# Output-projection weight sums formed in DRAM during attention, and no subtraction of weight parts on POOL

## The chip, the cores and the metric

The kernel runs on one core of a Trainium2 chip. The metric is the device time of one execution in microseconds (us); the runs before the change have a median of 803.27 us. One further execution was taken with the hardware profiler; all views below come from it. Engine names: PE is the matrix engine (PEld its weight load), DVE the vector engine, ACT the scalar engine, POOL the general engine, SP the one that only issues transfers. Transfers issued by SP run on queue q1, those issued by POOL on queue q0; both queues share 16 DMA engines.

## The reference, cut to what matters

A hybrid decoder layer for 512 tokens of width 1024: an mLSTM branch and a sparse-attention branch, merged by gates into `y`, an output projection with a residual, then a gated conv-MLP. The change concerns the output projection's weights:

```
y = sigmoid(gm + merge_gate_b[0]) * (hm @ w_up_m) + sigmoid(gn + merge_gate_b[1]) * (on @ w_up_n)
x = x + y @ w_out                      # w_out is 1024 x 1024
h2 = rmsnorm(x, norm2_w)
a, v = jnp.split(h2 @ ffn_w_up, 2, axis=-1)
a = jax.nn.gelu(causal_dwconv(a, ffn_conv_w, ffn_conv_b), approximate=False)
return x + (a * v) @ ffn_w_down
```

## The kernel before, in words

**Products.** Every float32 product is made of three matmuls of a reduced type (fp32r): with each operand split into a high part H and a low part L (the rest), it adds H·H, H·L and L·H (lines 507 to 509 in `mm3`; 567 to 569 in the feature-major projections, 587 to 589 in `up_group`). So every weight is loaded raw, copied to its high part on ACT (L102), and its low part is raw minus high. The class `Weights` does this in halves of 128x1024, in program order. A low half is made in one of four ways: by DVE (L110), by POOL (L110, for the halves in `on_pool`), late by DVE (L53), or, for the halves in `on_dma`, by a second ACT copy with the sign turned (L107) and an accumulating transfer issued by POOL that adds the raw weights to it (L108). Raw weights go through two buffers (`raw`), parts through a ring of four (`whl`); `rawdst` and `dst` give a chunk a place of its own, and `deep` lets one more chunk be loaded ahead.

**Stages.** First the input projections and attention: the rest of the projections (`proj_stream`: gates `gm`, output gates `mo`, `mqk`, gates `gn`) is fed between the pieces of attention and of the mLSTM by `fill`, so that PE always has matmuls. Attention is a loop over 32 pairs of a token tile and a head. Then `un` and `um` multiply the two branches by `w_up_n` and `w_up_m` (8 groups each of 12 matmuls), and their evacuations `evac_un` and `evac_um` on DVE merge them into `gm`, which then holds `y`.

**Output projection.** It takes 7 products of half-size blocks instead of 8. The blocks of `w_out` (512 x 512) are combined before use: T1 = w00 + w01, T2 = T1 + w11, T4 = T2 + w10, T3 = w01 + w11. The activations are combined likewise (s2, s5, s3, s7). PE runs the products in the order P1 (weights w00), P2 (w10), P6 (T2), P5 (T1), P3 (w11), P7 (T3), P4 (T4); each is 24 matmuls. Between them ACT and DVE split activations (`a_split`, L1457 and L1458), POOL adds products into the residual tiles `x` (L1585 to L1610), and DVE and ACT form the second norm (`norm2_sq`, `norm2_x` with the scaling L1561), whose result `junk` PE transposes (`pn`, L491) between P7 and P4. After P4 the first up-projection group (`ff`) begins.

**The sums before.** `wo_sums`, called in the mLSTM's last head, loads the four blocks into four pages of SBUF (L1359, tiles b11, b12, b22, b21) and forms the sums in place by 8 accumulating transfers issued by POOL (L1364). b11 then holds T1, b12 T3, b22 T2, b21 T4. `t_split` splits T1 and T2 while `um` runs (two ACT copies, L1462 and L1464, and an accumulating transfer on POOL's queue, L1465). T3 and T4 are split by `Weights`. POOL subtracts the low halves of the second half of T4 and of the first two up-projection halves (`LOWS`).

**What sets the order.** Each engine runs its instructions in the order of the program text; a wait stops everything behind it on that engine, and transfers of one queue are issued in order. Nothing is reordered by a planner; the table `PLAN` gives amounts of filler and engine choices, and the change does not touch it.

Of the kernel before, what the change touches and what calls it, by code (L numbers as in the profile page):

```python
# [15 lines left out]
P = 128  # L16
# [129 lines left out]
def FL(key, default):  # L146
    return PLAN.get(key, default)
# [30 lines left out]
def body(ctx, tc, I, out, dbg=None):  # L178
# [38 lines left out]
    def page_r(name):  # L217
        return page(name, F32R)
# [4 lines left out]
    def s4(name, dt=F32):  # L223
        return ar.tile([P, 1024], dt, name=name, tag="s4", bufs=6)
# [16 lines left out]
    def act4(tiles, k, a=0, b=S):  # L241
        return v4(tiles[k // 4])[:, k % 4, a:b]

    T = {}
    done = set()

    def cp(key, default, dst, src):
# [41 lines left out]
    def wo_block(r, c):  # L289
        return w_out[r * 512:r * 512 + 512, c * 512:c * 512 + 512].rearrange("(k p) n -> p k n", p=P)  # L290

    WB = {}
    for nm, rc, pg in (("b11", (0, 0), None), ("b21", (1, 0), None), ("b22", (1, 1), None), ("T3", None, "b12"),
                       ("T4", None, "b21")):
        W.deep.add(len(W.chunks))
        if pg:
            W.rawdst[len(W.chunks)] = lambda name, pg=pg: T[pg]
        WB[nm] = W.add((4, 512), [] if pg else [(lambda v: v, wo_block(*rc))],
                       [lambda v, a=a: v[:, a:a + 2] for a in (0, 2)])
    F_FA, F_FV = [], []  # L300
    for c in range(0, DFF, 256):
# [555 lines left out]
    def evac_un(m, a):  # L857
        g = T["gn"][m // 4][:, m % 4, :]
        dve.tensor_mul(g, g, a)
# [204 lines left out]
    def att_out(i, acc):  # L1064
# [6 lines left out]
        act.activation(oh, av, AF.Copy)  # L1071
        dve.tensor_sub(ol, av, oh)

    def attention():
        its = [(i, h) for i in range(NT) for h in range(8)]
        f1 = [FL(f"f1_{k}", v) for k, v in enumerate((1950, 1300, 1000, 1000)) for _ in range(8)]
        f2 = [FL(f"f2_{k}", v) for k, v in enumerate((0, 0, 1300, 1300)) for _ in range(8)]
        f3 = [FL(f"f3_{k}", v) for k, v in enumerate((650, 1000, 300, 300)) for _ in range(8)]
        pcs = {0: pc0}
        rows, step = rows_b(), None  # L1080
        sv, nmx = att_scores(0, 0)
        Pt, Pv, den = att_exp(0, 0, sv, nmx)
        fill(FL("z7", 1950))
        att_scale(0, 0, Pv, den)
        acc = po("on0")
        cmp_out(acc, pcs[0])
        fill(FL("z9", 1300))
        for n, (i, h) in enumerate(its):
            nxt = its[n + 1] if n + 1 < len(its) else None
            if nxt:  # L1090
# [36 lines left out]
            if nxt:  # L1127
                Pt, Pv, den = nPt, nPv, nden
# [222 lines left out]
    fill.until(done, "CONV")  # L1351
    assert "ROWS" in done

    def wo_sums():

        blocks = (("b11", (0, 0)), ("b12", (0, 1)), ("b22", (1, 1)), ("b21", (1, 0)))
        for nm, rc in blocks:
            T[nm] = opage(nm)
            nc.sync.dma_start(T[nm].rearrange("p (k n) -> p k n", k=4), wo_block(*rc))  # L1359
        for d, src in (("b11", (0, 1)), ("b12", (1, 1)), ("b22", "b11"), ("b21", "b22")):  # L1360
            dv = T[d].rearrange("p (k n) -> p k n", k=4)
            sv = T[src].rearrange("p (k n) -> p k n", k=4) if isinstance(src, str) else wo_block(*src)
            for k in (0, 2):
# [73 lines left out]
    x1p = [lpage("x1_0")]  # L1437
    x1 = [x1p[0][:, t * 1024:(t + 1) * 1024] for t in range(2)]
    s7t = s4("s7t")
    TH = {nm: [s4(f"{nm}H{i}", F32R) for i in range(2)] for nm in ("T1", "T2")}  # L1440
    nw2 = s4("nw2")

    A = {nm: page_r("A" + nm) for nm in ("a11", "a12")}
    TL = {nm: page_r(nm + "L") for nm in ("T1", "T2")}
    LO, HI = slice(0, 256), slice(256, 512)

    def Y(g, k0, n, t):  # L1450
# [6 lines left out]
        act.activation(h, src, AF.Copy)  # L1457
        dve.tensor_sub(l, src, h)  # L1458

    def t_split(nm, i):  # L1460
        src = T["b11" if nm == "T1" else "b22"][:, i * 1024:i * 1024 + 1024]
        act.activation(TH[nm][i], src, AF.Copy)  # L1462
        l = TL[nm][:, i * 1024:i * 1024 + 1024]
        act.activation(l, TH[nm][i], AF.Copy, scale=-1.0)  # L1464
        pool.dma_start(l, src, accum_op=ALU.add)  # L1465

    S7 = s7t.rearrange("p (k t) -> p k t", k=4)

    def s52(e, k0):
        e.tensor_sub(Y(0, k0, 2, HI), Y(0, k0, 2, HI), Y(1, k0, 2, HI))  # L1470
        e.tensor_sub(Y(0, k0, 2, LO), Y(0, k0, 2, LO), Y(0, k0, 2, HI))

    def evac_um(m, a):
        g = T["gm"][m // 4][:, m % 4, :]
        dve.tensor_mul(g, g, a)
# [133 lines left out]
    for a in range(2):  # L1609
        pool.tensor_sub(xh(2 + a, 0), xh(2 + a, 0), V[a])  # L1610
    A["a22"] = page_r("Aa22")
    for k in range(4):
        for a in range(2):
            wo("P5", a, (k,))
        if k == 1:
            norm2_sq(0, 0, 0)
            norm2_sq(1, 0, 0)
        elif k == 2:
            a_split("a22", Y(1, 0, 4, HI), 0, 4)
            for a in range(2):  # L1620
                norm2_e(a)
    for a in range(2):
# [24 lines left out]
    for a in range(2):
# [345 lines left out]
```

## Time and profile before

| | |
|---|---|
| median of 3 runs | 803.27 us (802.63 to 804.4) |
| the profiled execution | 802.46 us |
| its span, first to last instruction | 800.8 us |
| mean granted PE clock | 0.981 |
| PE busy | 771.3 us (96%) |
| DVE, ACT, POOL busy | 490.8, 393.0, 246.8 us |
| DMA | 140.56 MB, of it 45.09 MB on q0 |

Times in a view are us from the span's start, mean durations of one instruction ns. A row of the chain of waits gives start, duration and what filled it; a row of the timeline adds shapes, a count and in brackets the idle time before with its releaser; a row of the table of stretches gives busy time (and count) of each engine, the granted PE clock, the mean busy share of the 16 DMA engines and GB/s. A busy PE is not PE at its peak: at half the granted clock a matmul takes twice as long and still counts as busy.

### The profile page before, as it was taken

The numbers are of one execution on the slowest core, as the hardware profiler recorded it, in microseconds if no ns is written. First come the engines' busy times: TensorE is split into PE (matmuls) and PEld (weight loads), VectorE is DVE, ScalarE is ACT, GpSimd is POOL, SyncE is SP. The second block draws the span as 40 slices with busy tenths as digits, with TensorE's granted clock in tenths as the row PEclk, the third lists the DMA queues.
The fourth block names the chain that finished last, engine by engine and source line by source line (L and its number), as shares of the span: only waits on it lengthen the run. The fifth ranks groups of instructions, "written<-read, shape, count | busy, mean of one in ns | idle before, by whom it ended". The sixth has DMA issues, their size and how long they took to land.

```text
span 800.8 us, 10584 instructions
## 1 busy us (share of the span) xinstructions
PE 771.3 (96%) x3991; PEld 637.5 (80%) x3991; DVE 490.8 (61%) x844; ACT 393.0 (49%) x655; POOL 246.8 (31%) x251
## 2 busy tenths in 40 slices
PE   8999999999999999978876999999999999999998
PEld 7897887788888778867665988888888888888786
DVE  7486876776557575436558745554554544565866
ACT  6363565555565765746373443333333333355452
POOL 3320221210111222123348008855554443200600
PEclk9999999999999999997988999999999999999999
DMA  7974278755564577699983467675555444585472
GB/s 237 322 185 132 34 154 143 145 99 99 87 128 66 103 158 132 188 275 253 289 211 66 154 234 262 230 256 210 191 177 191 182 155 157 189 284 184 129 230 102
DMA packets 99459, 140.56 MB, mean 176 GB/s; under 512 B 6831, under 2 KB 72783, under 8 KB 98000
## 3 DMA queue, kind: packets, MB, share of 16 engines
q1 hardware_dynamic: 65662, 94.66, 35.3%
q0 software_dynamic: 33600, 45.09, 27.5%
q8 instruction: 31, 0.51, 0.3%
q14 instruction: 20, 0.16, 0.1%
q10 hardware_dynamic: 146, 0.14, 0.0%
HBM read 100.03 MB, written 15.73 MB: 145 GB/s over the span
## 4 chain that ended last, share of the span: by engine, by line
PE 85%; DMA 6%; DVE 4%; ACT 2%; issue 2%; POOL 0%; DVEq 0%; ACTq 0%; SPq 0%; POOLq 0%
PE ff L1676 10%; PE ff L1678 10%; PE ff L1677 10%; PE P L508 4%; PE P L509 4%; PE P L507 4%; DMA raw<-in_w_up_m_dram 3%; PE on L1061 3%; PE ptp L1050 2%; PE gn L567 2%; PE gm L567 2%; PE gm L569 2%; PE gm L568 2%; PE gn L569 2%; PE gn L568 2%; DMA raw<-in_w_out_dram 2%
## 5 line engine op out<-in xcount | busy, mean ns | idle before, releaser
L110 DVE TENSOR_TENSOR whl<-raw,whl 128x1024 fp32r<-128x1024 f32 (+1 forms) x102 | 132.0, 1304 | 144.8 <-ACT whl L102 144.6
L102 ACT ACTIVATE whl<-raw 128x1024 fp32r<-128x1024 f32 (+2 forms) x142 | 143.1, 1012 | 138.0 <-PE ff L1678 55.7
L1676 PE MATMUL ff<-h2H,whl 128*128 128x512 f32 (+1 forms) x376 | 141.3, 376 | 0.0
L1677 PE MATMUL ff<-h2L,whl 128*128 128x512 f32 (+1 forms) x376 | 141.2, 375 | 0.0
L1678 PE MATMUL ff<-h2H,whl 128*128 128x512 f32 (+1 forms) x376 | 141.2, 375 | 0.0
L108 POOL DMA_DIRECT2D whl<-raw x35 | 48.7, 1390 | 206.7 <-ACT whl L107 182.0
L1678 PEld LDWEIGHTS ff<-h2H,whl 128*128 128x128 f32 x376 | 70.8, 188 | 12.9
L1677 PEld LDWEIGHTS ff<-h2L,whl 128*128 128x128 f32 x376 | 70.8, 188 | 12.8
L1676 PEld LDWEIGHTS ff<-h2H,whl 128*128 128x128 f32 x376 | 70.8, 188 | 12.6
L1035 ACT ACTIVATE P<-sp,nmx 128x128 f32<-128x128 f32 (+3 forms) x64 | 33.1, 523 | 36.7 <-DVE nmx L1026 36.2
L1743 ACT ACTIVATE ct<-ct 128x512 f32<-128x512 f32 x22 | 13.9, 633 | 53.8 <-DVE ct L1741 53.8
L107 ACT ACTIVATE whl<-raw 128x1024 fp32r<-128x1024 f32 x35 | 36.7, 1049 | 0.0
L1026 DVE TENSOR_REDUCE nmx<-sp 128x2 f32<-128x256 f32 (+3 forms) x32 | 26.2, 819 | 16.3 <-PE sp L1023 16.2
L507 PE MATMUL P<-whl,g 128*128 128x512 f32 x88 | 34.2, 389 | 0.0
L508 PE MATMUL P<-whl,g 128*128 128x512 f32 x88 | 34.2, 389 | 0.0
L509 PE MATMUL P<-whl,g 128*128 128x512 f32 x88 | 34.2, 389 | 0.0
L1741 DVE SCALAR_TENSOR_TENSOR ct<-ff,vcol,ct 128x511 f32<-128x511 f32 (+1 forms) x44 | 32.7, 743 | 2.2 <-ACT ct L1739 1.4
L1749 ACT ACTIVATE g<-ct 128x512 fp32r<-128x512 f32 x22 | 13.9, 632 | 36.4 <-DVE ct L1753 21.4
L252 DVE COPY P<-ptp 128x256 f32<-128x256 f32 (+1 forms) x32 | 17.7, 553 | 18.4 <-PE ptp L1050 18.3
L1750 DVE TENSOR_TENSOR g<-ct,g 128x512 fp32r<-128x512 f32 x22 | 15.4, 699 | 21.9 <-ACT g L1749 21.9
L508 PE MATMUL P<-whl,sb 128*128 128x512 f32 (+1 forms) x68 | 26.3, 386 | 1.5 <-DVE whl L110 1.4
L567 PE MATMUL gm<-hTH,whl 128*128 128x512 f32 x64 | 26.6, 416 | 0.0
(453 smaller groups left out, 1847.7 us busy)
## 6 DMA issues: line engine op xcount, KB each, us to landing
raw<-in_ffn_w_up_dram SPq DMA_DIRECT2D x22, 1024.0 KB, 5.2
whl<-raw POOLq DMA_DIRECT2D x35, 512.0 KB, 5.7
raw<-in_w_in_dram SPq DMA_DIRECT2D x16, 1024.0 KB, 5.1
st<-in_ffn_w_down_dram SPq DMA_DIRECT2D x11, 1024.0 KB, 7.7
td<-st POOLq DMA_DIRECT2D x11, 1024.0 KB, 4.2
raw<-td SPq DMA_DIRECT2D x22, 512.0 KB, 5.5
raw<-in_ffn_w_down_dram SPq DMA_DIRECT2D x11, 512.0 KB, 3.9
b<-in_w_out_dram SPq DMA_DIRECT2D x4, 1024.0 KB, 8.1
```

The costliest lines, as they stand in the source:

```text
L102: nc.scalar.activation(h, src, AF.Copy)
L107: nc.scalar.activation(l, src, AF.Copy, scale=-1.0)
L108: nc.gpsimd.dma_start(l, src, accum_op=ALU.add)
L110: (nc.gpsimd if n in self.on_pool else nc.vector).tensor_sub(l, src, h)
L507: pe.matmul(o, aH, bH, start=start, stop=False)
L508: pe.matmul(o, aH, bL, start=False, stop=False)
L509: pe.matmul(o, aL, bH, start=False, stop=stop)
L567: pe.matmul(acc, H[:, k, :], hh, start=(k == 0), stop=False)
L1035: act.activation(Pv[:, y], sv[:, y], AF.Exp, bias=nmx[:, y:y + 1], accum_out=den[:, y:y + 1])
L1676: pe.matmul(acc[:, a:b], H[:, k, :], hh, start=(k == 0), stop=False)
L1677: pe.matmul(acc[:, a:b], H[:, k, :], hl, start=False, stop=False)
L1678: pe.matmul(acc[:, a:b], L[:, k, :], hh, start=False, stop=(k == KD - 1))
```

## The change

- **Sums in DRAM.** Four DRAM tiles `tw` (tags wT1 to wT4) take the sums. In each of the first 16 steps of attention SP copies a quarter of a block, 128 rows of 512 numbers, from DRAM to DRAM; in steps 4 to 19 POOL issues an accumulating transfer that adds a quarter of another block, or of an earlier sum, to it (`block_sums`). The 4 loads of L1359 and the 8 accumulating transfers of L1364 go. `wo_sums` now only loads T1 and T2; T3 and T4 are loaded by `Weights` as raw chunks into pages.
- **T1 and T2** are split by one ACT copy and one DVE subtraction each half, without a transfer, and earlier: T1 after `un` groups 2 and 3, T2 after `un` group 6 and `um` group 0.
- **No low halves on POOL.** Those of T4's second half and of the first two up-projection halves are made by the second ACT copy and an accumulating transfer. T4's parts get two pages of their own (`W.dst`), outside the ring, so the parts after them move up in the ring.
- **Places.** T4's halves are made before P5 and in P5, the two up-projection halves in P3 and in the second norm. The two subtractions of `s52` for the first features go from POOL to DVE.

```
-    for nm, rc, pg in (("b11", (0, 0), None), ("b21", (1, 0), None), ("b22", (1, 1), None), ("T3", None, "b12"),
-                       ("T4", None, "b21")):
-        W.deep.add(len(W.chunks))
-        if pg:
-            W.rawdst[len(W.chunks)] = lambda name, pg=pg: T[pg]
-        WB[nm] = W.add((4, 512), [] if pg else [(lambda v: v, wo_block(*rc))],
+    tw = {nm: dram.tile([P, 2112], F32, name="w" + nm, tag="w" + nm) for nm in ("T1", "T2", "T3", "T4")}
...
+    for nm, rc in (("b11", (0, 0)), ("b21", (1, 0)), ("b22", (1, 1)), ("T3", None), ("T4", None)):
+        if nm != "b11":
+            W.deep.add(len(W.chunks))
+        if not rc:
+            W.rawdst[len(W.chunks)] = lambda name: opage(name)
+        WB[nm] = W.add((4, 512), [(lambda v: v, wo_block(*rc) if rc else twv(nm))],
...
-    LOWS = (WB["T4"][1], F_FA[0], F_FA[1])
-    W.on_pool = {T_B[c] for c in range(4) if FL(f"q2_pb{c}", (1, 0, 0, 0)[c])} | set(LOWS)
+    W.on_pool = {T_B[c] for c in range(4) if FL(f"q2_pb{c}", (1, 0, 0, 0)[c])}
...
-                    ("UN", F_UN), ("UM", F_UM), ("WO", WB["b11"] + WB["b21"][:1] + WB["b22"] + WB["T3"] + WB["T4"][:1])):
+                    ("UN", F_UN), ("UM", F_UM), ("WO", WB["b11"] + WB["b21"][:1] + WB["b22"] + WB["T3"] + WB["T4"] + F_FA[:2])):
...
+    for i in WB["T4"]:
+        W.dst[i] = page_r
...
+        if m in (2, 3, 6):                                   # in evac_un
+            t_split("T2" if m == 6 else "T1", m % 2)
...
+    def block_sums(n):                                       # called at the start of attention's step n
+        names = ("T1", "T3", "T2", "T4")
+        k = n % 4
+        if n < 16:
+            nc.sync.dma_start(twv(names[n // 4])[:, k], wo_block(*((0, 0), (0, 1), (1, 1), (1, 0))[n // 4])[:, k])
+        if 4 <= n < 20:
+            z = n // 4 - 1
+            src = (wo_block(0, 1), wo_block(1, 1), twv("T1"), twv("T2"))[z]
+            pool.dma_start(twv(names[z])[:, k], src[:, k], accum_op=ALU.add)
...
+    def t_split(nm, i):
...
+        act.activation(TH[nm][i], src, AF.Copy)
+        dve.tensor_sub(TL[nm][:, i * 1024:i * 1024 + 1024], src, TH[nm][i])
...
     def wo_sums():
-        blocks = (("b11", (0, 0)), ("b12", (0, 1)), ("b22", (1, 1)), ("b21", (1, 0)))
-        for nm, rc in blocks:
+        for nm in ("T1", "T2"):
             T[nm] = opage(nm)
-            nc.sync.dma_start(T[nm].rearrange("p (k n) -> p k n", k=4), wo_block(*rc))
-        for d, src in (("b11", (0, 1)), ("b12", (1, 1)), ("b22", "b11"), ("b21", "b22")):
...
-                pool.dma_start(dv[:, k:k + 2], sv[:, k:k + 2], accum_op=ALU.add)
+            nc.sync.dma_start(T[nm], tw[nm][:, 0:2048])
...
-        act.activation(l, TH[nm][i], AF.Copy, scale=-1.0)    # the old t_split
-        pool.dma_start(l, src, accum_op=ALU.add)
...
         elif m == 5:                                         # in evac_um
-            t_split("T2", 1)
-            s52(pool, 0)
+            s52(dve, 0)
...
+    W.ensure(WB["T4"][0])                                    # before P5; T4[1] in P5 after k == 2,
     for k in range(4):                                       # the first up-projection half in P3 after k == 1,
         for a in range(2):                                   # the second in the second norm
             wo("P5", a, (k,))
```

In the order fences the number in a name is that of its buffer or tile: whl48 and whl49 are w00's parts, whl50 and whl51 w10's, 52 and 53 w11's, 54 and 55 T3's, 56 and 57 T4's, 58 and 59 the first two up-projection halves.

The first place is POOL from the last low half of `w_up_n` to the loads of the residual tiles, that is the `un` and `um` stage; before:

```order
L108 DMA whl41_3291<-raw20_3051 128x4x256
L1364 DMA b11_3390<-in_w_out_dram 128x2x512 x2
L1364 DMA b12_3392<-in_w_out_dram 128x2x512 x2
L1364 DMA b22_3394<-b11_3390 128x1024 x2
L1364 DMA b21_3396<-b22_3394 128x1024 x2
L1465 DMA T1L_3559<-b11_3390 128x1024
L1480 TENSOR_TENSOR s7t_3551<-gm0_1198 128x512
L1465 DMA T1L_3559<-b11_3390 128x1024
L108 DMA whl48_3612<-raw24_3523 128x1024
L1485 TENSOR_TENSOR s7t_3551<-gm0_1198 128x512
L1465 DMA T2L_3560<-b22_3394 128x1024
L108 DMA whl49_3654<-raw24_3523 128x1024
```

and of the change:

```order
L108 DMA whl41_3327<-raw20_3087 128x4x256
L1493 TENSOR_TENSOR s7t_3587<-gm0_1202 128x512
L108 DMA whl48_3636<-raw24_3554 128x1024
L1497 TENSOR_TENSOR s7t_3587<-gm0_1202 128x512
L108 DMA whl49_3675<-raw24_3554 128x1024
L108 DMA whl50_3715<-raw25_3634 128x1024
L1522 DMA x1_0_3586<-in_x_dram 128x1024 x2
L1522 DMA x1_1_3756<-in_x_dram 128x1024 x2
```

Eleven accumulating transfers ahead of w00's second half (whl49) are gone from POOL's queue, and with the later T2L transfer and the two `s52` subtractions nothing stands between w10's half and the residual loads.

The second place is POOL at the end of the output projection, from the last residual subtraction to the stores of the residual; before:

```order
L1610 TENSOR_TENSOR x1_1_3734<-x1_1_3734,V_3862 128x512 x2
L108 DMA whl56_3927<-b21_3396 128x1024
L110 TENSOR_TENSOR whl57_3954<-b21_3396,whl57_3954 128x1024
L110 TENSOR_TENSOR whl58_3982<-raw29_3804,whl58_3982 128x1024
L110 TENSOR_TENSOR whl59_3997<-raw29_3804,whl59_3997 128x1024
L1564 DMA x1d_3549<-x1_0_3550 128x1024 x2
```

and of the change:

```order
L1620 TENSOR_TENSOR x1_1_3756<-x1_1_3756,V_3886 128x512 x2
L108 DMA whl56_3899<-raw28_3782 128x1024
L108 DMA whl57_3931<-raw28_3782 128x1024
L108 DMA whl58_3959<-raw29_3828 128x8x128
L108 DMA whl59_3993<-raw29_3828 128x8x128
L1574 DMA x1d_3585<-x1_0_3586 128x1024 x2
```

Three subtractions on POOL have become three accumulating transfers in the same place of its queue.

The third place is POOL in attention, where whl20 to whl23 are low halves of the gates `gm`, whl24 and whl25 of `mo`, and wT1, wT3 and wT2 are the DRAM sums; before:

```order
L108 DMA whl20_1311<-raw10_1159 128x8x128
L108 DMA whl21_1406<-raw10_1159 128x8x128
L108 DMA whl22_1506<-raw11_1309 128x8x128
L108 DMA whl23_1597<-raw11_1309 128x8x128
L108 DMA whl24_1693<-raw12_1504 128x8x128
L1172 TENSOR_SCALAR mrowC_1734<-onesf_98 32x512
L108 DMA whl25_1790<-raw12_1504 128x8x128
```

and of the change:

```order
L108 DMA whl20_1317<-raw10_1163 128x8x128
L1091 DMA wT1_85<-in_w_out_dram 128x512
L108 DMA whl21_1416<-raw10_1163 128x8x128
L1091 DMA wT1_85<-in_w_out_dram 128x512 x3
L108 DMA whl22_1522<-raw11_1315 128x8x128
L1091 DMA wT3_87<-in_w_out_dram 128x512 x2
L108 DMA whl23_1617<-raw11_1315 128x8x128
L1091 DMA wT3_87<-in_w_out_dram 128x512 x2
L108 DMA whl24_1717<-raw12_1520 128x8x128
L1192 TENSOR_SCALAR mrowC_1758<-onesf_102 32x512
L1091 DMA wT2_86<-wT1_85 128x512 x2
L108 DMA whl25_1818<-raw12_1520 128x8x128
```

One to three adding transfers now stand between two low halves, and each waits for its copy, which stands behind a raw load in SP's queue.

More of the change, by code (lines that the diff above doesn't have):

```diff
@@ L242, in act4 @@
         return v4(tiles[k // 4])[:, k % 4, a:b]
-    T = {}
+    T, TH, TL = {}, {}, {}
     done = set()
@@ L292, in body, with twv @@
     WB = {}
-    for nm, rc, pg in (("b11", (0, 0), None), ("b21", (1, 0), None), ("b22", (1, 1), None), ("T3", None, "b12"),
-                       ("T4", None, "b21")):
-        W.deep.add(len(W.chunks))
-        if pg:
-            W.rawdst[len(W.chunks)] = lambda name, pg=pg: T[pg]
-        WB[nm] = W.add((4, 512), [] if pg else [(lambda v: v, wo_block(*rc))],
+    tw = {nm: dram.tile([P, 2112], F32, name="w" + nm, tag="w" + nm) for nm in ("T1", "T2", "T3", "T4")}
+    def twv(nm):
+        return tw[nm][:, 0:2048].rearrange("p (k n) -> p k n", k=4)
+    for nm, rc in (("b11", (0, 0)), ("b21", (1, 0)), ("b22", (1, 1)), ("T3", None), ("T4", None)):
[4 more added lines that the diff above has]
+        WB[nm] = W.add((4, 512), [(lambda v: v, wo_block(*rc) if rc else twv(nm))],
                        [lambda v, a=a: v[:, a:a + 2] for a in (0, 2)])
@@ L1089, in attention @@
             nxt = its[n + 1] if n + 1 < len(its) else None
+            block_sums(n)
             if nxt:
@@ L1352, in body @@
     assert "ROWS" in done
+    def t_split(nm, i):
+        if not i:
+            TH[nm] = [s4(f"{nm}H{z}", F32R) for z in range(2)]
+            TL[nm] = page_r(nm + "L")
+        src = T[nm][:, i * 1024:i * 1024 + 1024]
+        act.activation(TH[nm][i], src, AF.Copy)
+        dve.tensor_sub(TL[nm][:, i * 1024:i * 1024 + 1024], src, TH[nm][i])
     def wo_sums():
-        blocks = (("b11", (0, 0)), ("b12", (0, 1)), ("b22", (1, 1)), ("b21", (1, 0)))
-        for nm, rc in blocks:
+        for nm in ("T1", "T2"):
             T[nm] = opage(nm)
-            nc.sync.dma_start(T[nm].rearrange("p (k n) -> p k n", k=4), wo_block(*rc))
-        for d, src in (("b11", (0, 1)), ("b12", (1, 1)), ("b22", "b11"), ("b21", "b22")):
-            dv = T[d].rearrange("p (k n) -> p k n", k=4)
-            sv = T[src].rearrange("p (k n) -> p k n", k=4) if isinstance(src, str) else wo_block(*src)
-            for k in (0, 2):
-                pool.dma_start(dv[:, k:k + 2], sv[:, k:k + 2], accum_op=ALU.add)
+            nc.sync.dma_start(T[nm], tw[nm][:, 0:2048])
     T["mq"] = [v4(page_r(f"mq{p}")) for p in range(2)]
@@ L1439, in body @@
     s7t = s4("s7t")
-    TH = {nm: [s4(f"{nm}H{i}", F32R) for i in range(2)] for nm in ("T1", "T2")}
     nw2 = s4("nw2")
     A = {nm: page_r("A" + nm) for nm in ("a11", "a12")}
-    TL = {nm: page_r(nm + "L") for nm in ("T1", "T2")}
     LO, HI = slice(0, 256), slice(256, 512)
@@ L1458, in a_split @@
         dve.tensor_sub(l, src, h)
[L1460 to L1463, printed above, removed]
-        act.activation(l, TH[nm][i], AF.Copy, scale=-1.0)
-        pool.dma_start(l, src, accum_op=ALU.add)
     S7 = s7t.rearrange("p (k t) -> p k t", k=4)
@@ L1477, in evac_um @@
         if m == 0:
-            t_split("T1", 0)
+            t_split("T2", 1)
         elif m == 1:
             pool.tensor_sub(S7[:, 0:2], Y(0, 0, 2, HI), Y(0, 0, 2, LO))
-            t_split("T1", 1)
         elif m == 2:
@@ L1486, in evac_um @@
             a_split("a11", Y(0, 2, 2, LO), 2, 2)
-            t_split("T2", 0)
         elif m == 5:
-            t_split("T2", 1)
-            s52(pool, 0)
+            s52(dve, 0)
         elif m == 6:
@@ L1621, in body @@
                 norm2_e(a)
+            W.ensure(WB["T4"][1])
     for a in range(2):
@@ L1629, in body @@
         if k == 1:
-            W.ensure(WB["T4"][0])
+            W.ensure(ff_ids(0)[0])
     for a in range(2):
@@ L1635, in body @@
         norm2_x(a)
-        if not a:
-            W.ensure(WB["T4"][1])
+        if a:
+            W.ensure(ff_ids(0)[1])
     h2H = [opage_r(f"h2H{i}") for i in range(2)]
@@ L1643, in body @@
                 wo("P7", a, (k,))
-        W.ensure(ff_ids(0)[i])
     for t in range(2):
```

## The prediction

> **What bounds the kernel now.** First the page's busy rows, then what PE waited for.
>
> ```profile
> PE 771.3 (96%) x3991; PEld 637.5 (80%) x3991; DVE 490.8 (61%) x844; ACT 393.0 (49%) x655; POOL 246.8 (31%) x251
> ```
>
> ```profile
> PE pn L491 <- DVE junk L1561: 7.6, 2, 7.2
> PE um L587 <- DVE gn L859: 6.9, 1, 6.9
> PE wP L508 <- DMA whl<-raw: 3.4, 2, 2.1
> PE wP L509 <- DVE As L1458: 2.6, 1, 2.6
> PE wP L507 <- ACT As L1457: 1.6, 1, 1.6
> ```
>
> PE is the bound with 771.3 of 800.8 us. Nearly all its idle time is in these five rows, 22.1 us (total us, times, longest), and all five lie between `un` and the up-projection. So the table of stretches for that part, cut at the waits: `um` waits in the first row, runs in the next two, then P1 and P2, P6 alone, P5, P3 and P7, and last the second norm's transposes with P4.
>
> ```profile
> 355.90:362.90 7.00, 0.11 (x2) 0.03 (x1) 1.90 (x3) 2.96 (x4) 0.00 (x0) 0.66 1.09 259
> 362.90:368.30 5.40, 5.40 (x13) 4.24 (x14) 2.94 (x4) 3.05 (x3) 0.86 (x1) 0.50 1.04 288
> 368.30:384.60 16.30, 16.30 (x73) 13.48 (x72) 11.09 (x14) 11.49 (x13) 10.02 (x11) 1.00 1.07 231
> 384.60:401.10 16.50, 13.12 (x49) 9.99 (x48) 7.75 (x10) 2.62 (x4) 4.55 (x6) 0.90 1.04 313
> 401.10:406.60 5.50, 5.50 (x25) 4.33 (x24) 1.22 (x1) 4.65 (x5) 0.88 (x1) 1.00 0.51 153
> 406.60:418.90 12.30, 8.11 (x26) 6.05 (x25) 8.91 (x11) 9.42 (x16) 6.45 (x7) 0.72 0.99 214
> 418.90:430.00 11.10, 11.04 (x49) 8.82 (x47) 8.33 (x14) 6.05 (x13) 11.10 (x9) 1.00 0.32 75
> 430.00:447.30 17.30, 10.14 (x40) 8.46 (x41) 15.32 (x17) 4.75 (x10) 8.43 (x7) 0.70 0.51 153
> ```
>
> Columns: length, busy time with count of PE, PEld, DVE, ACT, POOL, then granted clock, DMA share, GB/s. Two things are to be seen. The DMA engines are full (share 1.04 to 1.09) up to 401. And each wait costs twice: after it the clock is halved (0.50, 0.90, 0.72, 0.70). At clock 1.00 a matmul takes 16.30 / 73 = 0.223 to 5.50 / 24 = 0.229; I use 0.226. From 355.9 to 447.3, 91.4 us, PE has 86 matmuls of `um` (13 + 73), 168 of the products and 16 small transposes (about 1.8 us), 59.2 us at full clock. So 32 us are waits and slow clock, the most that can be won.
>
> The chain of waits says what the waits hang on:
>
> ```profile
> 337.66 22.16 DMA raw<-in_w_up_m_dram
> 380.26 8.72 DMA whl<-raw
> 389.12 12.72 DMA raw<-in_w_out_dram
> 408.31 3.33 DVE As L1458
> 428.52 9.24 DVE junk L1561 x2
> 438.49 1.41 DVE junk L1561 x2
> ```
>
> `um` waits because its second weight chunk took 22.16 us to land; P1 and P2 because accumulated low halves came late; P5 because w11's raw chunk took 12.72, and ACT, which must split it first, was held. What filled the queues, with KB each and median us to landing:
>
> ```profile
> raw<-in_w_in_dram SPq DMA_DIRECT2D x16, 1024.0 KB, 5.1
> b<-in_w_out_dram SPq DMA_DIRECT2D x4, 1024.0 KB, 8.1
> b<-in_w_out_dram POOLq DMA_DIRECT2D x4, 512.0 KB, 14.9
> b<-b POOLq DMA_DIRECT2D x4, 512.0 KB, 11.5
> T1L<-b POOLq DMA_DIRECT2D x2, 512.0 KB, 10.0
> T2L<-b POOLq DMA_DIRECT2D x2, 512.0 KB, 8.7
> ```
>
> **The change, part by part.** *Sums moved.* 4 loads of 1 MB and 8 adding transfers of 0.5 MB leave the stretch 331 to 375, and so do the 4 of T1L and T2L. In their place come T1, T2 (1 MB each, at 331) and T3, T4 (behind w11's chunk). So `um`'s second chunk, still issued at 337.66, has 3 MB ahead instead of 5 and no adding queue beside it; at 259 to 313 GB/s that is 10 to 12 us from 330.6 plus its own 1 MB, 345 at the latest. It is needed at 350 or so. The wait of 6.9 goes, and with it the slow clock behind it: `um` runs from 355.9 for 86 x 0.226 = 19.4, to 375.3 instead of 384.6: **9.3 us**.
>
> *P1 and P2.* w00's second low half was issued at 380.26, 17.4 after `um` resumed; ACT had T1's and T2's copies ahead of it, POOL eleven transfers. Now it hangs on the release of its ring place, the end of `um`'s fourth group: 36 matmuls after 355.9, 8.1, then two DVE steps (0.7 each), an ACT split (0.6) and two ACT copies (1.05 each), 368.8. The next view, the tile's transfers on POOL's queue from 395 to 435, gives issue to landing:
>
> ```profile
> DMA to landing us min/median/max: 4.4/5.2/10.5
> ```
>
> With an empty queue I take the minimum, 4.4 (bounds 4.4 and 8.72): 373.2. P1 needs it at 378, P2's first low half comes some 3 us later for 381. The 16.5 of P1 and P2 becomes 48 x 0.226 = 10.9: **5.6 us**. P6 then ends at 375.3 + 72 x 0.226 = 391.6.
>
> *P5.* Here a wait stays. w11's chunk is issued when that low half has landed (380.26 + 8.72, then 12.72 before). Now it is issued at 373.2, beside 2 MB of residual loads and a low half of 0.5 MB: 3.5 MB at the 313 GB/s of that stretch, 11.7, so it lands at 385 (alone 5.1: 378; as before 12.72: 386). From there on the engines' order is that of before, and I carry its rows along, 17 us earlier:
>
> ```profile
> 401.95 1.06 ACT L102 ACTIVATE whl<-raw 128x1024 fp32r<-128x1024 f32 x1 [11.23 <-DMA raw<-in_w_out_dram]
> 407.65 0.62 ACT L1457 ACTIVATE As<-gm 128x512 fp32r<-128x512 f32 x1
> 408.21 2.85 POOL L1585 TENSOR_TENSOR x<-x,cp 128x512 f32<-128x512 f32 x2
> 408.31 3.92 DVE L1458 TENSOR_TENSOR As<-gm,As 128x512 fp32r<-128x512 f32 x2 [2.15 <-ACT As L1457]
> 426.84 2.56 POOL L1610 TENSOR_TENSOR x<-x,V 128x512 f32<-128x512 f32 x2
> 429.33 0.91 POOL L108 DMA_DIRECT2D whl<-b  x1
> 429.99 2.63 POOL L110 TENSOR_TENSOR whl<-b,whl 128x1024 fp32r<-128x1024 f32 x1
> 432.29 4.91 POOL L110 TENSOR_TENSOR whl<-raw,whl 128x1024 fp32r<-128x1024 f32 x2
> ```
>
> ACT takes the chunk at 385 and has P5's first split done 6.3 later, 391.3; DVE's low part is held while POOL adds (3.92 for two that take 0.69 each alone) and comes at 394.5, where before it came at 411.7. P5 thus waits 2.5 instead of 4.2 and stays the late one. P5, P3 and P7 end 28.0 after ACT took the chunk, as in before (430.0 - 401.95): 413.0, that is 21.4 after P6 instead of 23.4: **2.0 us**.
>
> *The second norm.* The pair of scalings L1561 took 9.24 in one tile and 1.41 in the other; the long one lies beside POOL's three subtractions of low halves (429.99 to 437.2). These go, so 1.41 holds for both: the transposes wait no longer. Late next is T4: its first low half stands behind L1610 on POOL, which ended 27.4 after ACT took the chunk, now 412.4; landing 4.4 later, 416.8. PE has P7's end and 8 transposes behind it at 413.9, so it waits 2.9, then 5 matmuls, 8 transposes, 18 matmuls (1.1 + 0.9 + 4.1), 422.9. Behind a wait of 2.09 the clock row shows 0.90 over 16.5, 3.3 us at half speed, 1.65 lost; I add that, 424.6. The up-projection's first low half, third in that queue, lands within 424 at 2.6 us for each half ahead. The last stretch becomes 11.6 instead of 17.3: **5.7 us**.
>
> *Costs off the path.* DVE gets 4 subtractions of 1.23 and 2 of 0.69; in `un` and `um` it is busy 11.09 of 16.30 at most. ACT loses 4 copies and gains 3. POOL's 16 adds and SP's 16 copies fall into attention, where:
>
> ```profile
> L108 POOL DMA_DIRECT2D whl<-raw x23 | 35.1, 1528 | 161.0 <-ACT whl L107 154.0 <-PE sp L1023 3.3 <-PE mhT L1291 2.1
> DMA to landing us min/median/max: 5.5/5.9/11.2
> 120.00:140.00 20.00, 20.00 (x121) 15.82 (x120) 12.91 (x45) 11.92 (x33) 3.54 (x3) 1.00 0.89 142
> 180.00:200.00 20.00, 20.00 (x142) 16.23 (x142) 12.02 (x32) 11.21 (x28) 1.54 (x1) 1.00 0.57 97
> ```
>
> From 110 to 330 POOL sat idle 161 us ahead of its 23 low halves, so 16 more issues of 0.9 to 1.5 (14 to 24 us) fit. A low half comes every 7 to 15 us, lands in 5.9 and is used two halves later, some 20 us. The adds' 4 MB in 90 us (46 GB/s) and the copies' 4 MB put the DMA share from 0.57 to 0.89 near 1 for a short while only. Behind an add that waits for its copy stands the next low half, whose slack is those 14 us or more. I cost attention at nothing: cover idle POOL and that slack; if it goes, PE starves for gate weights.
>
> The Trainium skill, "SBUF — State Buffer", section "SBUF: two separate sides", speaks against this part: an issue on POOL's queue can be held while DVE runs one of its two-port instructions, from some 620 to 3100 ns. By that the 16 adds would take some 50 us of POOL instead of 24 and still leave over 100 idle, so the sum stands. The row of 1528 ns on average, with DVE busy 12 of 20, shows no such hold so far.
>
> **The sum.** 9.3 + 5.6 + 2.0 + 5.7 = 22.6: the up-projection starts at 424.7 instead of 447.3, and behind it nothing changes. Span 800.8 - 22.6 = 778.2; the profiled execution took 802.46, 1.66 beyond its span, and lies 0.8 under the median, so **780.7** against 803.27.
>
> On the clock, the Trainium skill, "TensorE: Matmul & The Clock Gate", Part 1, has the rate halved only after an idle window of some 3.4 us. By that the remaining waits of 2.5 and 2.9 would cost no slow clock and the sum would be 778 (an estimate). The row 384.60:401.10, with waits of 1.29 and 2.09 and a clock of 0.90, contradicts it.
>
> **The rivals.** (A) *The low halves on the queue come late.* T4's and the up-projection's parts are four transfers in a row behind POOL's additions; at the longest landing seen, 10.5 instead of 4.4, the wait before P4 is 9.0, and the half clock 1.7 longer: 780.7 + 7.8 = 788.5. For it: the same queue took 8.7 to 14.9 when full; against: from 418.9 on the DMA share is 0.32 to 0.51. (B) *w11's chunk lands early* (5.1 alone): P5 starts at 391.6, no wait in P5 and one less slow window; 3 to 7 us more, 774 to 778. Against it: the residual loads are issued just ahead. (C) *Attention slower.* Each group of adds on POOL waits for copies and lands so late that the low half behind it misses its 14 us. It decides from some 17 us a group on: 7 groups, 3 us over each, are 21 us and eat the gain; at 20 us a group it is 42, so 803.3 - 22.6 + 42 = 823. For it: DRAM as the target of an adding transfer is shown nowhere in this trace, and adds took 14.9 in a full queue; against: shares of 0.57 and POOL's 161 idle us. (D) *The relief doesn't come*, because the engines refill with T3, T4, the up-projection's raws and the residual ahead of w11's chunk: only the first 9.3 and half the norm's 5.7 remain, 791; with `um`'s chunk late too, about 803.
>
> **How the numbers follow.** Forecast, 776.5 to 786: 0.60. A, 786 to 795: 0.17. B, 774 to 776.5: 0.09. D up to 801.6: 0.08, and within 0.2% of before: 0.02. C, slower: 0.04. A change within 0.2% can't be told from none here. Faster 0.94, same 0.02, slower 0.04. The range 775 to 791 takes in most of B and the nearer half of A, about 0.8.
>
> **What would show it.** Right: no wait of `um` on gn; `um`'s second chunk landing by 346; P1 and P2 without DMA waits; L1561 at about 1.4 a pair twice; DMA share below 1 between 340 and 372; no PE wait from 110 to 330. A wait of PE in P4 for a low half and one in P5 for As should be left, 2 to 3 us each. Wrong: a PE wait in attention, w11's chunk over 13 us, or P4 waiting over 6.

## The result, and the profile after

The changed kernel takes 781.43 us (median of 6 runs, 780.27 to 782.60) against 803.35: a ratio of 0.9726, 95% interval 0.9713 to 0.9739. The forecast was 780.7. The profiled execution took 782.1, its span is 780.4 (forecast 778.2). The total came out right, but not by its own sum: two of its four terms were too large, and two gains that it did not name made up for most of that. The profiled execution is the second slowest of the six, at a mean granted clock of 0.991 where the fastest (780.27) has 0.995, and its span gained 20.4 where the medians differ by 21.9.

The page's busy rows after, then all waits of PE behind attention (total us, times, longest):

```profile
PE 766.2 (98%) x3991; PEld 635.0 (81%) x3991; DVE 486.5 (62%) x850; ACT 392.0 (50%) x654; POOL 245.9 (32%) x253
```

```profile
PE wP L514 <- DMA whl<-raw: 2.8, 1, 2.8
PE wP L515 <- DVE As L1478: 2.8, 1, 2.8
PE wP L513 <- ACT As L1477: 2.0, 1, 2.0
PE um L593 <- DVE gn L865: 0.5, 1, 0.5
```

Idle time of 22.1 us has become 8.1, and each row is a wait of which the forecast speaks. (The first is in P4, the next two in P5; this kernel's L514, L515, L593 and L1478 are L508, L509, L587 and L1458 of before.) The table of stretches, columns as before: `un`, `um`, P1 and P2, P6, P5, P3 with P7, P4, and the first up-projection group.

```profile
331.00:356.50 25.50, 25.47 (x117) 20.82 (x115) 14.77 (x27) 20.57 (x30) 0.00 (x0) 1.00 0.57 206
356.50:375.80 19.30, 18.84 (x83) 15.62 (x84) 17.98 (x24) 9.10 (x11) 6.85 (x9) 1.00 0.50 123
375.80:386.80 11.00, 11.00 (x51) 9.09 (x50) 5.71 (x8) 2.62 (x4) 0.46 (x1) 1.00 1.02 321
386.80:392.30 5.50, 5.50 (x26) 4.49 (x24) 1.10 (x1) 4.09 (x5) 0.88 (x1) 1.00 1.01 414
392.30:406.60 14.30, 9.55 (x32) 7.12 (x31) 9.17 (x11) 11.32 (x18) 7.73 (x8) 0.76 1.07 265
406.60:417.70 11.10, 11.09 (x53) 8.86 (x51) 9.21 (x17) 8.37 (x15) 11.10 (x9) 1.00 0.22 69
417.70:426.90 9.20, 6.40 (x21) 5.13 (x20) 6.61 (x13) 3.50 (x8) 4.15 (x4) 0.63 1.20 181
426.90:432.00 5.10, 5.10 (x33) 4.58 (x32) 3.35 (x8) 3.40 (x9) 1.07 (x2) 1.00 1.19 331
```

The DMA share in `un` and `um` is 0.50 to 0.57, where it was 1.04 to 1.09, and `um`, P1 and P2 run at clock 1.00. The half clock is now behind P5's and P4's waits alone (0.76, 0.63). How long it lasts is not set by the wait alone. P4's wait of 2.8 comes with half clock for 6.83 us in this trace, and the same wait in `no_adds` (below) with half clock for 3.41, by the granted clock on record. The same 3.3 us of P4, here and in `no_adds`:

```profile
423.30:426.60 3.30, 3.30 (x13) 2.91 (x12) 2.38 (x5) 1.20 (x2) 0.00 (x0) 0.50 1.41 177
423.30:426.60 3.30, 3.30 (x19) 2.81 (x18) 2.46 (x4) 1.54 (x3) 0.20 (x1) 1.00 1.45 185
```

DVE is busy 17.98 of 19.30 us in `um`, which the forecast called free. The chain of waits names the links left:

```profile
370.43 4.43 DMA whl<-raw
374.99 13.12 DMA raw<-in_w_out_dram
394.58 2.47 DVE As L1478
413.27 2.48 POOL x L1620 x2
415.75 4.96 DMA whl<-raw
```

They are w00's second low half, w11's raw chunk, P5's operand, POOL's last subtraction, and T4's first low half behind it.

By the starts of the same matmuls in the two timelines (un's first matmul at 330.77 and 331.26, so 0.49 is lost ahead of it):

| stretch | before | after | gain | forecast |
|---|---|---|---|---|
| un to P1 | 53.85 | 44.87 | 9.0 | 9.3 |
| P1 and P2 | 16.53 | 10.88 | 5.65 | 5.6 |
| P6 to the second norm's transposes | 28.86 | 29.40 | -0.5 | 2.0 |
| transposes and P4, to the up-projection | 17.30 | 13.38 | 3.9 | 5.7 |
| up-projection | 242.85 | 242.07 | 0.8 | 0 |
| down-projection | 106.75 | 104.67 | 2.1 | 0 |

The up-projection starts at 429.79, where 424.7 was forecast. The last row is a wait that I overlooked in the trace of before. One row each of PE and DVE and two of POOL of before, then DVE's and one of POOL's of after:

```profile
756.21 0.50 PE L508 MATMUL P<-whl,sb 128*128 128x512 f32 x1 [1.39 <-DVE whl L110]
748.09 5.03 DVE L110 TENSOR_TENSOR whl<-raw,whl 128x512 fp32r<-128x512 f32 x1
746.96 0.55 POOL L1829 DMA_DIRECT2D out_dram<-x1r  x1 [1.94 <-DVE whl L110]
747.52 1.30 POOL L1889 TENSOR_TENSOR x1r<-x1r,V 128x512 f32<-128x512 f32 x1
```

```profile
729.78 1.08 DVE L110 TENSOR_TENSOR whl<-raw,whl 128x512 fp32r<-128x512 f32 x1
727.50 0.55 POOL L1840 DMA_DIRECT2D out_dram<-x1r  x1 [0.78 <-DVE x1r L1903]
```

Four of POOL's additions stand in a row there, spaced by 1.25, and in before DVE's low half came in only behind all of them: it took 5.03, and PE waited. In the changed kernel, where POOL's first addition starts 0.2 us earlier against DVE, the same low half came in behind the first and took 1.08. The down-projection takes 104.67 or 104.68 in every kernel of this study but the one before. The 0.2 us come from POOL's issue of a store ahead of the additions. In before it starts 1.46 after its data are ready (745.50), behind the end of another low half on DVE (746.64); in the changed kernel it starts 0.30 after its data (727.20), while that low half still runs. Why the issue waited for the low half in before alone stays open.

### The profile page after: what moved, and what is told of

Read it like the earlier page. It is cut to its first block, busy times and chain, and to the rows that moved or that the text cites. A ratio compares the mean times of both kernels' runs of the same rounds, so it can differ in the third digit from the quotient of the medians.

```text
span 780.4 us, 10620 instructions
## 1 busy us (share of the span) xinstructions
PE 766.2 (98%) x3991; PEld 635.0 (81%) x3991; DVE 486.5 (62%) x850; ACT 392.0 (50%) x654; POOL 245.9 (32%) x253
## 4 chain that ended last, share of the span: by engine, by line
PE 87%; DMA 4%; ACT 3%; DVE 3%; issue 2%; POOL 1%; POOLq 0%; ACTq 0%; DVEq 0%; SPq 0%
PE ff L1688 10%; PE ff L1687 10%; PE ff L1689 10%; PE P L513 4%; PE P L514 4%; PE P L515 4%; PE on L1069 3%; PE ptp L1058 2%; PE gn L573 2%; PE gm L575 2%; PE gm L573 2%; PE gm L574 2%; PE gn L575 2%; PE gn L574 2%; DMA raw<-in_w_out_dram 2%
## 5 line engine op out<-in xcount | busy, mean ns | idle before, releaser
L110 DVE TENSOR_TENSOR whl<-raw,whl 128x1024 fp32r<-128x1024 f32 (+1 forms) x102 | 130.3, 1287 | 135.3 <-ACT whl L102 135.1
L102 ACT ACTIVATE whl<-raw 128x1024 fp32r<-128x1024 f32 (+2 forms) x146 | 147.4, 1013 | 123.4 <-PE ff L1689 60.5
L108 POOL DMA_DIRECT2D whl<-raw x41 | 55.3, 1403 | 194.6 <-ACT whl L107 161.2
L107 ACT ACTIVATE whl<-raw 128x1024 fp32r<-128x1024 f32 x41 | 43.0, 1048 | 0.0
L1754 ACT ACTIVATE ct<-ct 128x512 f32<-128x512 f32 x22 | 13.9, 633 | 53.8 <-DVE ct L1752 53.8
L514 PE MATMUL P<-whl,g 128*128 128x512 f32 x88 | 34.2, 389 | 0.0
L515 PE MATMUL P<-whl,g 128*128 128x512 f32 x88 | 34.2, 389 | 0.0
L1760 ACT ACTIVATE g<-ct 128x512 fp32r<-128x512 f32 x22 | 13.9, 632 | 36.4 <-DVE ct L1764 21.4
L1761 DVE TENSOR_TENSOR g<-ct,g 128x512 fp32r<-128x512 f32 x22 | 15.4, 699 | 21.9 <-ACT g L1760 21.9
L514 PE MATMUL P<-whl,sb 128*128 128x512 f32 (+1 forms) x68 | 26.0, 383 | 0.0
```

The source lines that it names most:

```text
L102: nc.scalar.activation(h, src, AF.Copy)
L107: nc.scalar.activation(l, src, AF.Copy, scale=-1.0)
L108: nc.gpsimd.dma_start(l, src, accum_op=ALU.add)
L110: (nc.gpsimd if n in self.on_pool else nc.vector).tensor_sub(l, src, h)
L514: pe.matmul(o, aH, bL, start=False, stop=False)
L515: pe.matmul(o, aL, bH, start=False, stop=stop)
```

## The experiments

Each kernel is compared by the median of its runs with 781.43; the kernel before took 802.76 to 803.52 beside them. In 14 profiled executions un's first matmul lies between 330.77 and 332.38 with no relation to the edit, so stretches are compared from there.

**The parts apart.** `lows_only` is before with only this:

```
-    W.on_pool = {...} | set(LOWS)
+    W.on_pool = {...}
...
-  ... WB["T3"] + WB["T4"][:1])
+  ... WB["T3"] + WB["T4"] + F_FA[:2])
```

> The kernel before, with only one part of the change: the low halves of T4's second half and of the first two up-projection halves are made by a second ACT copy and an accumulating transfer instead of by a subtraction on POOL. The sums stay in SBUF. Theory: POOL's three subtractions hold the scaling L1561; without them the pair takes about 1.4 instead of 9.24, the wait of 7.15 before the second norm's transposes goes, and a wait of 2 to 3 us for T4's first low half takes part of it: 803.3 - 5.7 = 797.6 (797 to 799). Rival: the scaling is slow for another reason, or the low halves come as late on the full queue: no gain, 803.

795.33 us (ratio 0.9898, 0.9883 to 0.9913). `lows_on_pool` is the changed kernel with these lines put back.

> The changed kernel, with those three low halves made by POOL's subtraction again; the sums stay in DRAM. Theory: the norm's scaling is held again (about 9 for the pair), a PE wait of some 7 us before the second transposes returns and the wait of 2.8 for T4's first low half goes: 781.4 + 5.7 = 787 (785 to 789). Rival: with T4's halves made earlier the subtractions lie beside P5 and P3 and cost nothing: 781.

788.72 us (0.9819, 0.9802 to 0.9835). The scaling L1571 (L1561 of before), POOL's subtractions beside it, PE's wait (`lows_on_pool`), and then the wait that is left in P4 in `lows_only`:

```profile
415.80 9.25 DVE L1571 SCALAR_TENSOR_TENSOR junk<-x,uoc,nw 128x512 f32<-128x512 f32 x2
417.28 7.21 POOL L110 TENSOR_TENSOR whl<-raw,whl 128x1024 fp32r<-128x1024 f32 x3
PE pn L497 <- DVE junk L1571: 8.7, 2, 7.1
```

```profile
PE wP L508 <- DMA whl<-b: 2.3, 1, 2.3
```

The subtractions cause the norm's wait, shown from both sides. The parts add up to within 1 us: taking away POOL's subtractions gives 8.2 from before (803.52 beside it) and 7.3 with the rest of the change made; the rest gives 14.8 and 13.9. The 2.1 of the down-projection are in 8.2 and in 14.8 alike, since either part alone brings them. `lows_only` won more than expected: up to the up-projection the stretch from un is 6.0 shorter (116.54 to 110.57), as priced, and the 0.8 and 2.1 of the last two table rows are in it too.

**Attention.** `no_adds` leaves the 16 adding transfers out.

```
-            pool.dma_start(twv(names[z])[:, k], src[:, k], accum_op=ALU.add)
```

> The changed kernel without the 16 adding transfers in attention; the 16 copies stay, so the sums hold single blocks (the output projection's result is another one). Theory: the adds cost attention nothing: un starts at 331.3 as with them, time 781.4 within 0.7. Rival: they cost a little in attention, and the time falls by 0.7 or more, with un earlier by as much.

781.08 us (0.9721, 0.9707 to 0.9736), un at 330.81. The adds cost nothing that can be measured; the 16 copies stayed in, and no run leaves them out alone. In the changed kernel POOL's issues and two stretches of attention read:

```profile
L108 POOL DMA_DIRECT2D whl<-raw x23 | 35.5, 1543 | 146.4 <-ACT whl L107 130.6 <-PE gn L575 9.0 <-PE sp L1031 3.3
L1091 POOL DMA_DIRECT2D wT<-wT x8 | 9.9, 1757 | 0.0
L1091 POOL DMA_DIRECT2D wT<-in_w_out_dram x8 | 9.7, 1785 | 0.0
120.00:140.00 20.00, 20.00 (x122) 15.86 (x120) 12.87 (x45) 11.97 (x33) 6.65 (x6) 1.00 1.10 217
180.00:200.00 20.00, 20.00 (x136) 16.17 (x137) 11.62 (x31) 11.16 (x27) 3.31 (x3) 1.00 0.88 158
```

The 16 issues take 19.6 us of POOL's idle time (estimated 14 to 24), and PE is busy throughout although the DMA share rose to 1.10.

**What relieved the queue.** `tsplit_dma` splits T1 and T2 by transfer again, in the new places.

```
-        dve.tensor_sub(TL[nm][:, i * 1024:i * 1024 + 1024], src, TH[nm][i])
+        l = TL[nm][:, i * 1024:i * 1024 + 1024]
+        act.activation(l, TH[nm][i], AF.Copy, scale=-1.0)
+        pool.dma_start(l, src, accum_op=ALU.add)
```

> The changed kernel, with T1's and T2's low parts made as before by a second ACT copy and an accumulating transfer on POOL's queue, in the new places. Theory: the transfers lie in the stretch of un and um, where the DMA share is now 0.5 to 0.6, and cost nothing; the four copies fall into ACT's idle time but for about one: 781.4 + 0 to 1. Rival: it was these four transfers, not the sums' twelve, that kept the queue full before, and the waits of um, P1 and P2 come back in part: 785 or more.

779.27 us (0.9703, 0.9687 to 0.9719): neither theory, it is 2.2 less, an amount at the edge of what these intervals part. The four transfers, in their new places, fill no queue, which leaves the sums' twelve. For `um`'s wait the trace of before rules the four out directly: the second chunk was under way from 337.66 to 359.82, beside the sums, and the first of the four was issued only at 369.28. Two rows of POOL in before:

```profile
338.78 4.89 POOL L1364 DMA_DIRECT2D b<-in_w_out_dram  x4 [12.47 <-DMA b<-in_w_out_dram]
369.28 1.20 POOL L1465 DMA_DIRECT2D T1L<-b  x1
```

For P1 and P2, what the sums' going and what the earlier splits are each worth is not shown: no run keeps the sums and only moves the splits. As for the 2.2, the traces point to DVE: in the changed kernel its four subtractions of 1.23 put the merge behind in `um`. PE's wait on `gn` (0.48) is gone, w00's second low half is issued at 369.00 instead of 370.43, and ACT takes w11's chunk at 385.99 instead of 388.21. POOL's and ACT's rows of `tsplit_dma`:

```profile
369.00 0.87 POOL L108 DMA_DIRECT2D whl<-raw  x1 [1.47 <-ACT whl L107]
385.99 1.06 ACT L102 ACTIVATE whl<-raw 128x1024 fp32r<-128x1024 f32 x1 [6.31 <-DMA raw<-in_w_out_dram]
```

**P5's wait.** Three edits. `x1_early` moves half the residual's loads:

```
+    for t in range(2):                       # ahead of um
+        pool.dma_start(x1[t], x[t * P:(t + 1) * P, :])
...
-    for t in range(NT):
+    for t in range(2, NT):
```

> The changed kernel with the first half of the residual (two loads of 0.5 MB) loaded ahead of um instead of ahead of P1. Theory: w11's raw chunk took 13.12 because 2 MB of residual and the low half shared the DMA engines with it; with 1 MB less it lands some 3 us earlier, P5's first wait goes and the second shrinks to about 1.7: 781.4 - 3 to 5 = 776.5 to 778.5. Rival: the chunk is slow for another reason, and neither wait nor time moves: 781.4.

`s5_first` splits w11 and T3 later:

```
-        W.ensure(WB["b22"][i])               # in P1's loop
...
         a_split("s5", Y(0, 2 * i, 2, HI), 2 * i, 2)
-        W.ensure(WB["T3"][i])
+    W.ensure(WB["b22"][1])                   # behind P2
+    W.ensure(WB["T3"][1])
```

> The changed kernel with the splits of w11 and T3 behind both splits of P5's operand in the program, so that ACT no longer waits for w11's raw chunk ahead of them. Theory: P5 waits (1.99 and 2.76) only because ACT is held by that chunk, which takes 13.12 to land, and the half clock that follows costs some 2 more; all go, and w11's low halves still land ahead of P3: 781.4 - 5 = 776 (774 to 778). Rival: w11's parts are then late for P3, or the norm behind it is held in another place, and the wait only moves: 780 to 783.

`cp_dve` takes two additions from POOL:

```
-        pool.tensor_add(xh(a, 0), xh(a, 0), cp1[a])
...
+        dve.tensor_add(xh(a, 0), xh(a, 0), cp1[a])   # behind P2
         wo_add(a, 0, "P2")
```

> The changed kernel with POOL's two additions of the copied P1 product made by DVE, behind P2. Theory: P5's second wait (2.76) is DVE's subtraction for its operand, held by those two additions on POOL (2.47 where one takes 0.69 alone); it falls to under 0.5, and the half clock after it goes: 781.4 - 4.5 = 777 (776 to 779.5). Rival: the subtraction is slow for another reason, or DVE's own two additions give it back: 781 to 782.

They took 778.97 (0.9701, 0.9685 to 0.9718), 779.34 (0.9700, 0.9685 to 0.9714) and 782.81 us (0.9744, 0.9730 to 0.9759). The chunk in `x1_early` (chain), the waits of PE in `s5_first`, then in `cp_dve`:

```profile
375.35 10.71 DMA raw<-in_w_out_dram
```

```profile
PE wP L514 <- DMA whl<-raw: 3.3, 2, 2.1
PE pn L497 <- DVE junk L1571: 2.4, 1, 2.4
```

```profile
PE pn L497 <- DVE junk L1571: 3.8, 1, 3.8
PE wP L514 <- DMA whl<-raw: 1.9, 1, 1.9
```

With 1 MB less beside it the chunk takes 10.71 instead of 13.12, and P5's first wait goes: the residual held it. In `s5_first` both waits of P5 go, in `cp_dve` the one of 2.76 goes, each cause as expected. The times fell short of what was expected, for 2.4 and 3.8 come back as a wait for the second norm, which the changed kernel does not have: `s5_first` keeps 2.1, `cp_dve` nothing. So P5's wait had covered the norm's own chain; in `cp_dve` DVE's two additions also stand in that chain, and the two were not told apart.

**P4's wait.** `t4_first` moves T4's splits ahead of POOL's additions, `v_dve` makes those additions on DVE.

```
+    W.ensure(WB["T4"][0])                    # t4_first: behind P2; T4[1] behind P6
...
-        pool.tensor_add(xh(a, 1), xh(a, 1), V[a])    # v_dve, and five more, and the scaling of nw2
+        dve.tensor_add(xh(a, 1), xh(a, 1), V[a])
```

> The changed kernel with T4's two halves split earlier: the first behind P2, the second behind P6, so that their accumulating transfers stand ahead of POOL's additions of V in its queue instead of behind L1620. Theory: P4's wait of 2.80 goes and with it the half clock that follows it for 5.7 us, worth 2.9: 781.4 - 5.7 = 775.7 (775 to 777). Rival 1: the clock is halved there whatever PE waits for: only 2.8 is won, 778.6. Rival 2: the up-projection's first low half, now next in the queue, is late in its place: 779 to 781.

> The changed kernel with POOL's six additions of V and its scaling of the norm's weights made by DVE. Theory: T4's low halves no longer stand behind them on POOL, P4's wait of 2.80 and the half clock after it (2.9) go; DVE has some 5 us more, of which about 1 delays the second norm: 781.4 - 4.7 = 776.7 (775 to 778.5). Rival: DVE, busy 18 of 25 there, makes the norm later by as much as is won, and the transposes wait: 780 to 783.

`t4_first` took 784.13 us (0.9761, 0.9746 to 0.9775), slower than the changed kernel and beyond both rivals. P4 no longer waits; PE waits for the norm instead. PE's waits in it, DVE's split of P4's operand with POOL's additions beside it, and the same split in the changed kernel:

```profile
PE pn L497 <- DVE junk L1571: 4.3, 2, 2.9
408.56 6.08 DVE L1478 TENSOR_TENSOR Aa<-gm,Aa 128x1024 fp32r<-128x1024 f32 x1 [2.18 <-ACT Aa L1477]
407.21 2.85 POOL L1617 TENSOR_TENSOR x<-x,V 128x512 f32<-128x512 f32 x2
409.71 2.84 POOL L1619 TENSOR_TENSOR x<-x,V 128x512 f32<-128x512 f32 x2
```

```profile
407.20 2.19 DVE L1478 TENSOR_TENSOR Aa<-gm,Aa 128x1024 fp32r<-128x1024 f32 x1 [2.18 <-ACT Aa L1477]
```

Two transfers issued in between moved POOL's additions by 1.35 us against DVE, and DVE's split, 1.22 alone, took 6.08 instead of 2.19; the whole norm is 4 us later. `v_dve` took 781.56 us (0.9731, 0.9713 to 0.9748). From P1 to the up-projection it is 47.91 instead of 53.66: 5.75 won, the price set on P4's wait and its slow clock. The up-projection gives back 3.5 (245.59 instead of 242.07), waiting for the third tile's norm. The 2.25 that this trace leaves do not show in the medians, which agree, as the rival had it.

**Together.** `best_a` is `s5_first`, `x1_early` and `v_dve`, with `cp_dve`'s two additions ahead of P2; `best_b` adds this:

```
-    ff_mm(accs[0], ff_ids(0)[0], 0, 256, range(0, 6))
+    ff_mm(accs[0], ff_ids(0)[0], 0, 256)
+    ff_mm(accs[1], ff_ids(0)[1], 0, 256, range(0, 4))
     pn2 = [norm_tp(2, junks[2], pf(f"pn2_{g}"), g) for g in range(2)]
...
```

> The changed kernel with four moves together: the splits of w11 and T3 behind both splits of P5's operand; the first half of the residual loaded ahead of um; POOL's additions of V and its scaling on DVE; the two additions of the copied P1 product on DVE, ahead of P2. POOL then only issues transfers there. Theory: the waits of P5 and of P4 go together with their half clock (4.75 + 1.9 and 2.8 + 2.9), since nothing of the second norm's chain stands beside POOL any more; the up-projection gives back 3.5, as when V's additions alone were moved, because the third tile's norm is late: 781.4 - 12.3 + 3.5 = 772.6 (770 to 775). Rival: the chain behind the second norm has a length of its own, and each us won ahead of it turns into a wait of the transposes: 776 to 778.

> The same four moves, and in the up-projection 18 more matmuls of 256 columns ahead of the third tile's transposes (6 of the first group and 12 of the second). Theory: the wait of about 2 before these transposes is covered, with its slow clock: 3 us less than without, 769.6 (767.5 to 772). Rival: the second group's low half or the fourth tile then comes late, and the time stays where it is.

774.51 us (0.9645, 0.9631 to 0.9659) and 774.13 (0.9643, 0.9625 to 0.9660): both beat the changed kernel by some 7 us, and cannot be told apart, so the 3 us expected of `best_b`'s order did not come: in its trace PE waits 0.8 for a late low half and 0.7 for an operand of the up-projection instead. PE's waits in `best_a`:

```profile
PE pn L497 <- DVE junk L1573: 3.2, 2, 1.8
PE um L593 <- DVE gn L865: 0.5, 1, 0.5
```

All waits of the products are gone; P1 to the up-projection takes 43.69. `best_c` adds `tsplit_dma`'s edit to `best_b`, and puts the splits of P3's operand between those of w11:

```
+    for i in range(2):                       # behind P2
+        W.ensure(WB["b22"][i])
+        s3_sub(2 * i)
+        a_split("s3", Y(1, 2 * i, 2, LO), 2 * i, 2)
...
```

> The four moves with the up-projection's changed order, and two more: T1's and T2's low parts by a second ACT copy and an accumulating transfer again (DVE is then not behind in um), and the splits of P3's operand put between the two splits of w11, so that DVE no longer stands idle for 6.4 us behind ACT's splits of w11 and T3 and then makes the additions of V late. Theory: the second norm is on time, the wait of 1.5 before its first transposes and the 0.5 in um go, the waits of 0.3 to 0.8 in the up-projection in part: 774.1 - 2.5 = 771.6 (770 to 773). Rival: the second norm's chain is bound by its own latency behind P3 and the waits stay: 773.5 to 774.5.

777.97 us (0.9686, 0.9671 to 0.9701), slower than `best_b`. Its one large wait of PE, and the links of the chain ahead of it:

```profile
PE wP L514 <- DMA whl<-raw: 6.3, 1, 6.3
358.68 16.02 DMA raw<-in_w_out_dram
377.09 11.10 DMA whl<-raw
```

T2's two adding transfers and the early residual loads now fall together at 357 to 360, ahead of w10's chunk. It takes 16.02, its low half 11.10, and P2 waits 6.3: the kernel before in small. T2's transfers alone, in the same place, do not do it: in `tsplit_dma` P1 and P2 take 10.88. The residual's loads alone were not tried there: in `x1_early` they are issued at 332, since POOL has no transfers of T1 and T2 ahead of them.

## Why the prediction was right or wrong

- *um, 9.3, and P1 and P2, 5.6.* Right: 9.0 and 5.65. The full queue was the cause; for `um` the sums filled it, for P1 and P2 that is argued from `tsplit_dma`. What is missing from 9.3 comes from the wait of 0.48 on `gn`. One bound was worked out wrongly, to no effect: `um`'s second chunk was to land by 345 at the latest, where the lower of the rates used gives 346.8 (4 MB at 259 GB/s from 330.6). Measured, the DMA engines stand still from 344 on.
- *P5, 2.0.* Wrong: -0.5. "ACT takes the chunk at 385" was the step that failed: it was 388.2. The order behind it was carried along rightly: from there to the transposes 28.2 us, forecast 28.0. The prediction's own sign for this, w11's chunk over 13 us, came. The chunk came late for two reasons. The low half that releases it was issued at 370.43 instead of 368.8 (the steps named for 368.8 add up to 368.1), mostly because DVE's subtractions for T1 and T2, booked under "costs off the path" at nothing, put DVE behind (`tsplit_dma`: 369.00). And the chunk took 13.12 instead of 11.7.
- *The second norm and P4, 5.7.* The mechanism was right, and shown by `lows_on_pool` and `lows_only`; the new wait was forecast at 2.9 and is 2.80. The size failed on the slow clock: 13.38 less the wait, 24 matmuls (5.4) and 16 transposes (1.8) leaves 3.4 us, half of the 6.83 at half clock, where 1.65 was taken from a row with half clock for 3.41. The longer one is not a matter of the wait: in `no_adds` the same wait comes with 3.41, and the same part takes 11.88, close to the 11.6 forecast. So whether this term came out was luck, and a range of 1.7 to 3.4 would have been the sound one.
- *Attention at nothing.* Right, `no_adds`. The Trainium skill's rule on a held issue ("SBUF — State Buffer", "SBUF: two separate sides") did not show: low halves are issued in 1543 ns on average, before 1528.
- *Behind the up-projection's start nothing changes.* Wrong: 0.8 and 2.1 came there. The wait of 1.39 at 756 stood in the trace of before; the forecast left it out under "nearly all", with the 2.1 that hung on it.
- *The sum.* 22.6 forecast up to the up-projection, 17.5 measured there with the 0.49 ahead of `un`; 2.9 not forecast made 20.4 of the span.
- *Rivals.* A did not come: the first low half landed in 4.96, and though the three behind it took 7.8 to 12.1, PE waited for none of them. Nor did C or D. B's early chunk did not come either; `s5_first`, where P5 does not hang on it, is worth 2.1, not 3 to 7, since the norm is next.
- *The clock.* By the Trainium skill ("TensorE: Matmul & The Clock Gate", Part 1) waits under an idle window of about 3.4 us would cost no slow clock. The stretches with 0.76 and 0.63 follow waits of 1.99 and 2.76 and of 2.80; the measurement decides.

## What to carry to other kernels

Read the waits of the bounding engine over the whole span before calling a sum complete, and give a moved instruction a price on the engine that takes it even where its busy share looks low. Where two engines hold each other, a wait that is removed shows what stood behind it: price the next late chain before the edit. Give the half clock behind a wait as a range, since the same wait cost 1.7 us in one trace and 3.4 in another. Spread transfers over stretches where the queue is not full, but not several edits into the same stretch.

## What the runs showed of the hardware

- One DVE instruction with two SBUF operands can be held over several POOL instructions in a row: 6.08 us for a split of 1.22, 5.03 for a low half that takes 1.08, 9.25 for a pair of 1.41. A shift of POOL against DVE by 1.35 us (the split) and by 0.2 (the low half) made the difference. The Trainium skill ("SBUF — State Buffer", "SBUF: two separate sides") has the loser of the shared port blocked for the other's whole instruction; here it was blocked for up to four.
- Wherever the granted clock fell to half in the 14 traces, up to the last matmuls, it did so for 3.41, 6.83 or 10.24 us. Single waits from 1.79 us (`best_a`) on could bring it, but it stayed full behind one of 2.06 (`v_dve`), one of 2.27 (`lows_only`) and all up to 1.69. The wait does not set the length: with P4's wait of 2.75 to 2.80 it was 3.41 in `no_adds` and `x1_early`, 6.83 in the changed kernel and in `tsplit_dma`.
- An adding transfer with DRAM as its target (0.25 MB) takes 7.1 to 15.2 us to land in attention, and POOL 1.77 us to issue; successive issues overlap, so that 16 take 19.6.
